# Memory attention in two rounds by token half, with the output projection in three passes, the first among the steps of the second round

## The chip, the cores and the metric

The kernel runs on one core of a Trainium2 chip. The metric is the device time of one launch in microseconds (us); a smaller one is better. A profiled execution gives, besides its own time, every instruction of the engines: PE (TensorE), DVE (VectorE), ACT (ScalarE), POOL (GpSimd), and SP, which issues the DMA transfers.

## The reference

One inference step of a hybrid decoder layer on 1024 prompt tokens and 8 x 4 = 32 sample tokens, 1056 columns in all, with D = 1024. The change concerns the middle of it:

```python
# prompt: mem_k, mem_v of 256 memory tokens computed by memory_kv; sample: cache_mem_k, cache_mem_v
h = rmsnorm(x, norm_mem)
qm = (h @ w_mq).reshape(bsz, seqlen, MEM_HEADS, MEM_HEAD_DIM)          # 4 heads of 256
s = jnp.einsum('blhd,bmhd->bhlm', qm, mem_k).astype(f32) * (MEM_HEAD_DIM ** -0.5)
pr = jax.nn.softmax(s, axis=-1).astype(x.dtype)
o = jnp.einsum('bhlm,bmhd->blhd', pr, mem_v).reshape(bsz, seqlen, D_MODEL)
x = x + o @ w_mo
h = rmsnorm(x, norm_ffn)
u = h @ w_up                                                           # start of the FFN
```

The 1024 prompt tokens share one memory of 256 tokens; each of the 8 sample sequences (4 tokens each) has a cached memory of its own, 2 MB of keys and 2 MB of values in two tiles of 512 KB each.

## The kernel before, in words

Activations lie transposed: channels on the 128 partitions, in eight tiles, tokens along the columns. Each product is made of three matmuls of rounded parts, high x high, high x low, low x high. The high part is written by ACT (`wh`, `s`), the low part by DVE (`wl`, `s`). Weights come in units of 128 x 512 (256 KB): one DMA into a raw tile (`wr`, three buffers), one ACT copy and one DVE subtraction (`wsplit`, L202). A list made ahead (`plains`, L213) fixes their order, and `next_unit` (L274) prepares one unit ahead of the one handed out. `tick` (L292) is called between matmuls and advances generators of side work (`background`), one step in so many ticks. All of it stands in program order on each engine, so that an instruction waits for those ahead of it on its engine. Every operation is issued by one helper, so all rows show line 84 (87 in the changed kernel).

PSUM has eight banks of 512 columns. `psum_mode` (L114) divides them anew for each part of the kernel: `mm` tiles of several banks for wide products, `hm` tiles of two banks with two small tiles `ms` in the attention and the output projection, eight `mb` tiles of one bank in the FFN.

**q.** Eight products (`mm_full`, L325) make q from `w_mq`, the last from 783 us on. Each is scaled by the norm into a tile `t` and split into two tiles (high, low) of 1056 columns. In the last two, K and V of head 0 are loaded and split (`load_kv`, L1065). `mask_q` spreads the sample tokens' q for the eight sequences.

**Attention.** A unit is one head and one half of 512 prompt tokens: scores s (`attn_scores`, L1180: 24 matmuls of 256 columns, then softmax along the memory, with the maximum and the scaling on DVE, the exponential on ACT), transposition t (`attn_tr`, L1198: 8 transposes, then the split), output o (`attn_out`, L1211: 12 matmuls of 512 columns, then the split into `oh`, `ol`). The sample tokens' attention is a generator of 20 steps x (`sample_attn`, L1111), of which 8 have 16 matmuls for scores against the cached keys and 8 have 16 for the outputs with the cached values; its tiles are loaded two steps ahead. The string `ATTN` sets the order of s, t, o, x; units go head by head, both halves of a head in a row, and K/V of the next head are loaded after the first half's scores.

**Output projection.** Two passes over 528 columns each, right half (`rh`, with the sample tokens), then left half (`lh`). Each takes all 16 units of `w_mo`, eight output tiles m of 48 matmuls with 264 columns (2 x 264 share a weight). Then x1 is added on DVE, the sum is stored (`scr_acc`) and squared on ACT, and the squares are added up on POOL. While the second pass runs, the right half's norm and the eight input parts of the FFN are made in the background (`inputs_rh`, L1285).

**FFN start.** `psum_mode(1, 0)`, then the products `up_rh(j)` of right-half inputs with one weight unit each, for the j of `EARLY`, 14 of them, while `inputs_lh` (L1329) makes the left half's inputs and the sums and differences that the later products need.

## Time and profile before

| | us |
|---|---|
| median of 3 runs | 1710.28 (1708.33 to 1710.48) |
| profiled execution | 1703.74 |
| its span | 1701.8 |
| PE busy | 1669.1 (98% of the span) |
| DVE, ACT, POOL busy | 1096.0, 808.1, 213.3 |

The span runs from the first to the last instruction that the profile shows. "Busy" for PE runs to the modelled end of pipelined matmuls. A timeline row's start is measured; the time from the start of one block to that of the next is what a block takes. The stages that the change touches are the end of the q products (to 795 us), the attention (795 to 876), the output projection (876 to 973.5) and the start of the FFN.

### The profile page before, as it was taken

What the parts mean: (1) busy time and instruction counts of PE and PEld (TensorE: products, weight loads), DVE (VectorE), ACT (ScalarE), POOL (GpSimd) and SP (SyncE); (2) the same over time, 40 slices, a digit from 0 to 9 for tenths busy, and PEclk for the clock granted to TensorE, in tenths of its full rate; (3) what the DMA queues carried; (4) which work ended last, traced back from release to release, by engine and by line L of the source; (5) the groups of instructions that cost most, each with busy time, mean ns of one, the idle gap of its engine ahead of it and who ended that gap; (6) DMA issues with size and microseconds to landing.
All of it is one profiled execution on the core that took longest, in us unless ns stands there. A gap on an engine that the chain in (4) does not pass through costs nothing.

```text
span 1701.8 us, 30903 instructions
## 1 busy us (share of the span) xinstructions
PE 1669.1 (98%) x12250; PEld 1600.4 (94%) x12250; DVE 1096.0 (64%) x1728; ACT 808.1 (47%) x1494; POOL 213.3 (13%) x376
## 2 busy tenths in 40 slices
PE   9999999999999999999999999999999999999997
PEld 8899989899889899998789999999999999999997
DVE  7766867787778654434644697847484746466576
ACT  7565533434523443223543465656465555555553
POOL 0110000001002000011001200232223221322210
PEclk9999999999999999999999999999999999999999
DMA  6243355444785654313655542483748373654732
GB/s 216 88 164 85 58 141 111 97 105 105 247 288 192 225 165 135 107 44 106 229 187 177 176 158 82 103 139 93 134 91 141 74 124 73 114 99 89 130 122 103
DMA packets 152162, 226.13 MB, mean 133 GB/s; under 512 B 39873, under 2 KB 77249, under 8 KB 152017
## 3 DMA queue, kind: packets, MB, share of 16 engines
q1 hardware_dynamic: 138192, 198.20, 38.8%
q0 software_dynamic: 13824, 25.96, 11.3%
q8 instruction: 96, 1.57, 0.4%
q14 instruction: 50, 0.40, 0.1%
HBM read 156.22 MB, written 67.89 MB: 132 GB/s over the span
## 4 chain that ended last, share of the span: by engine, by line
PE 84%; DMA 7%; DVE 6%; ACT 2%; issue 1%; SPq 0%; DVEq 0%; ACTq 0%
PE mb L84 40%; PE mm L84 30%; PE hm L84 7%; PE ms L84 6%; DVE s L84 3%; DMA s<-scr_acs 3%; ACT s L84 1%; DVE wl L84 1%; DMA wr<-w_mk 1%; DMA s<-xT 0%; ACT wh L84 0%; DMA ld<-kc 0%; SPq L84 0%; DMA ld<-o_v 0%; DMA wr<-w_mv 0%
## 5 line engine op out<-in xcount | busy, mean ns | idle before, releaser
L84 PE MATMUL mb<-s,wh 128*128 128x264 f32 x3616 | 662.6, 285 | 1.1 <-DVE s L84 0.9
L84 PEld LDWEIGHTS mb<-s,wh 128*128 128x128 f32 x3616 | 560.8, 188 | 1.9 <-ACT wh L84 1.4
L84 PE MATMUL mb<-s,wl 128*128 128x264 f32 x1808 | 511.7, 284 | 0.7 <-DVE wl L84 0.7
L84 PE MATMUL mm<-s,wh 128*128 128x352 f32 (+1 forms) x2624 | 509.1, 326 | 1.1 <-DVE s L84 0.9
L84 PEld LDWEIGHTS mm<-s,wh 128*128 128x128 f32 x2624 | 431.9, 188 | 7.6 <-DVE s L84 2.1
L84 PEld LDWEIGHTS mb<-s,wl 128*128 128x128 f32 x1808 | 340.4, 188 | 1.1 <-DVE wl L84 1.1
L84 ACT ACTIVATE wh<-wr 128x512 fp32r<-128x512 f32 (+1 forms) x252 | 153.3, 608 | 352.0 <-PE mm L84 213.4
L84 PE MATMUL mm<-s,wl 128*128 128x352 f32 (+1 forms) x1312 | 289.2, 322 | 0.6 <-DVE wl L84 0.6
L84 DVE TENSOR_TENSOR wl<-wr,wh 128x512 fp32r<-128x512 f32 (+1 forms) x252 | 167.8, 668 | 125.9 <-ACT wh L84 122.5
L84 PEld LDWEIGHTS mm<-s,wl 128*128 128x128 f32 x1312 | 224.8, 189 | 3.0 <-DVE wl L84 1.2
L84 DVE SCALAR_TENSOR_TENSOR t<-t,par 128x1104 f32<-128x1104 f32 (+4 forms) x132 | 169.6, 1297 | 34.7 <-ACT t L84 33.3
L84 ACT ACTIVATE s<-s 128x512 f32<-128x512 f32 (+8 forms) x138 | 94.1, 690 | 128.4 <-DVE s L84 64.1
L84 DVE TENSOR_TENSOR wl<-ws,wh 128x512 fp32r<-128x512 f32 x118 | 81.0, 689 | 103.9 <-ACT wh L84 103.7
L84 ACT ACTIVATE q<-mb 128x264 f32<-128x264 f32 x264 | 99.7, 384 | 92.5 <-PE mb L84 69.6
L84 POOL DMA_DIRECT2D scr_acc<-q x96 | 83.0, 864 | 198.0 <-ACT q L84 181.5
L84 DVE TENSOR_TENSOR s<-s 128x512 f32<-128x512 f32 (+9 forms) x102 | 82.0, 824 | 32.5 <-ACT s L84 31.1
L84 ACT ACTIVATE wh<-ws 128x512 fp32r<-128x512 f32 x118 | 73.9, 628 | 55.3 <-PE mb L84 49.1
L84 ACT ACTIVATE t<-mb 128x264 f32<-128x264 f32 x132 | 51.2, 389 | 73.6 <-PE mb L84 72.1
L84 PE MATMUL hm<-s,wh 128*128 128x264 f32 x512 | 84.0, 285 | 0.3 <-ACT s L84 0.3
L84 DVE TENSOR_TENSOR t<-mm,rbc 128x1056 f32<-128x1056 f32 (+4 forms) x51 | 45.6, 908 | 52.8 <-PE mm L84 52.2
L84 ACT ACTIVATE t<-t,par 128x1104 f32<-128x1104 f32 (+4 forms) x60 | 74.6, 1247 | 4.7 <-DVE t L84 1.7
L84 PEld LDWEIGHTS hm<-s,wh 128*128 128x128 f32 x512 | 71.1, 188 | 0.7 <-ACT s L84 0.5
(189 smaller groups left out, 1742.0 us busy)
## 6 DMA issues: line engine op xcount, KB each, us to landing
scr_acc<-q POOLq DMA_DIRECT2D x96, 264.0 KB, 4.3
ws<-w_up SPq DMA_DIRECT2D x66, 256.0 KB, 3.1
wr<-w_in SPq DMA_DIRECT2D x56, 256.0 KB, 2.9
wr<-w_up SPq DMA_DIRECT2D x36, 256.0 KB, 2.8
wr<-w_dn SPq DMA_DIRECT2D x48, 192.0 KB, 2.4
s<-scr_acs SPq DMA_DIRECT2D x33, 256.0 KB, 5.2
wr<-w_mo SPq DMA_DIRECT2D x32, 256.0 KB, 2.8
scr_pool<-t SPq DMA_DIRECT2D x8, 528.0 KB, 5.9
```

Source lines behind the costliest of these rows:

```text
L84: i = fn(*args, **kwargs)
```

## The change

**Order of the attention.** Units are ordered by token half: all four heads for prompt tokens 512 to 1023 (`lb` 1) first, then all four for tokens 0 to 511. The string has a fourth letter, m, a step of half an output tile of the projection's first pass. In the first round s and x fill between t and o, in the second m.

**Three passes.** The first pass (`mo_first`) takes the 512 prompt tokens whose outputs the first round has made: 8 tiles of 24 matmuls with 512 columns, as 16 steps m. The output tiles `oh`, `ol` hold these tokens in columns 0 to 511, then the 32 sample tokens, then tokens 0 to 511. The second pass takes columns 512 to 783, the third 784 to 1055, 24 matmuls of 272 columns per tile; the last tile's two units are kept from the second to the third, so that 46 units are loaded instead of 32. x1 comes in one transfer per tile, in the first pass.

**PSUM and buffers.** Eight one-bank `mb` tiles from the attention on, no second change before the FFN; scores, transposes and outputs are evicted bank by bank. High and low part of q lie in one tile per half. K and V of heads 0 to 2 are loaded and split within the last q products, head 3 after the third score unit. The cache tiles come from a table of pools (`CACHE_IN`), three steps ahead instead of two.

**Side work.** The squares are added on DVE instead of POOL. In the third pass only the tiles 4 to 7 of the FFN's right-half inputs are made, 0 to 3 behind it in `inputs_lh`. `EARLY` has one more product.

PE at the opening of the attention, from the last matmuls of the q products (`mm`) on. Sample steps are the groups of 32x256, a transposition 128x128 x8, an output unit 128x512 x12; of a row of sample steps only the beginning is shown. Before:

```order
L84 MATMUL mm<-s,wl 128x352 x3
L84 MATMUL hm<-kv,s 128x256 x24
L84 MATMUL ms<-ld,sq 32x256 x2
L84 MATMUL ms<-ld,s 32x256 x2
...
L84 MATMUL hm<-kv,s 128x256 x24
L84 MATMUL ms<-t,sq 32x256 x2
L84 MATMUL ms<-t,s 32x256 x2
...
L84 MATMUL hm<-cst,p 128x128 x8
L84 MATMUL hm<-s 128x256 x24
```

In the changed kernel:

```order
L87 MATMUL mm<-s,wl 128x352 x3
L87 MATMUL mb<-kv,s 128x256 x24
L87 MATMUL mb<-s 128x256 x24
L87 MATMUL mb<-ld,qm 32x256 x10
L87 MATMUL mb<-s,qm 32x256 x2
...
L87 MATMUL mb<-cst,p 128x128 x8
L87 MATMUL mb<-s 128x256 x24
L87 MATMUL mb<-s,kv 128x512 x12
```

The second score unit has moved ahead of the first sample step, two sample steps stand ahead of the first transposition instead of three, and from there a score unit stands between a transposition and its output unit.

PE at the end of the attention. Before, the last transposition, sample steps, the last output unit, the sample outputs' transposes (`os_`), and the projection's first matmuls (weights `wh`, `wl`):

```order
L84 MATMUL hm<-cst,p 128x128 x8
L84 MATMUL ms<-ld,s 32x256 x8
L84 MATMUL ms<-t,s 32x256 x8
L84 MATMUL hm<-s 128x512 x12
L84 MATMUL ms<-cst,os__8472 128x128 x2
L84 MATMUL hm<-s,wh 128x264 x7
L84 MATMUL hm<-s,wl 128x264 x2
```

In the changed kernel, the beginning of the second round (the fifth unit's output is the row with `kv`, `pm` are the sample tokens' probabilities):

```order
L87 MATMUL mb<-s,wh 128x512 x2
L87 MATMUL mb<-s,wl 128x512
L87 MATMUL mb<-s,kv 128x512 x12
L87 MATMUL mb<-s 128x256 x24
L87 MATMUL mb<-t,pm 32x256 x8
L87 MATMUL mb<-ld,pm 32x256 x8
L87 MATMUL mb<-cst,p 128x128 x8
```

Matmuls of the projection now stand, like sample steps before, between a transposition and the next output unit, and the second round's units and steps stand between matmuls of the projection.

DVE in the projection: the lower parts of the weight units (`wl`) and the adds of x1 (`s<-hm,t`, `s<-mb,s`). Before, at its beginning (128x32 are the sample outputs' low parts):

```order
L84 TENSOR_TENSOR wl<-wr,wh 128x512
L84 TENSOR_TENSOR s<-ms,s 128x32 x2
L84 TENSOR_TENSOR s<-hm,t 128x528
L84 TENSOR_TENSOR wl<-wr,wh 128x512 x2
L84 TENSOR_TENSOR s<-hm,t 128x528
```

In the second pass of the changed kernel:

```order
L87 TENSOR_TENSOR wl<-wr,wh 128x512
L87 TENSOR_TENSOR s<-mb,s 128x32
L87 TENSOR_TENSOR s<-mb,s 128x240
L87 TENSOR_TENSOR wl<-wr,wh 128x512
L87 TENSOR_TENSOR s<-s,t 128x528
L87 TENSOR_TENSOR s<-s,t 128x240
```

The square sums (`s<-s,t`) have come to DVE between the splits, and the add comes in two pieces.

The diff, cut to its core:

```diff
-EARLY = (*range(13), 21)
+EARLY = (*range(14), 21)
-ATTN = "sxsxxt" + "sxoxt" * 3 + "sxotsxotsxot" + "xxoxxtxxxo"
+ATTN = "ssxxtsotxxsotxxsotxxsoxt" + "mxmosxxtmmmosxxtmmmoxxtmmmoxxmxmmxmm"
+CACHE_IN = ("ll", "lS", "SS", "SS", "ll", "lT", "Tl", "ll", "TT", "ll", "lT", "Tl", "ll", "TT", "ll", "lT")
+IN_EVERY = 3
+RH_LAG = 4
-    for nm in ("w_out_y", "w_mq", "w_mo", "w_mo"):
-        plains(A[nm][m, h] for m in range(8) for h in range(2))
+    for nm, n in (("w_out_y", 8), ("w_mq", 8), ("w_mo", 8), ("w_mo", 8), ("w_mo", 7)):
+        plains(A[nm][m, h] for m in range(n) for h in range(2))
...
     for m in range(8):
         if m == 6:
-            load_kv(0)
+            kvr[0] = kv_raw(0)
         ps = mm_full(KT, hh, hl)
+        if m == 6:
+            split_kv(0, kvr[0])
+            kvr[1] = kv_raw(1)
+        if m == 7:
+            split_kv(1, kvr[1])
+            nxt.append(cache(0, 0))
+            kvr[2] = kv_raw(2)
+            split_kv(2, kvr[2])
+            kvr[3] = kv_raw(3)
         t = ttile()
         V.tensor_tensor(v3(t), ps[:, :, :BW], v3(rbs[0]), op=ALU.mult)
...
-        hi, lo = split(t[:, :T])
+        for lb in (1, 0):
+            src = t[:, lb * 512:(lb + 1) * 512]
+            qt[m][lb] = q = stile(F32R)
+            S.activation(q[:, :512], src, AF.Copy)
+            V.tensor_tensor(q[:, 512:1024], src, q[:, :512].bitcast(F32), op=ALU.subtract)
...
-            nxt.append(cache(b >= 6, (b + 2) % 8))
+            nxt.append(cache(b >= 5, (b + 3) % 8))
...
+    def mo_first():
+        for m in range(8):
+            ps = mbtile()
+            mo(ps, 0, slice(0, 512))
+            yield
+            t = stile()
+            dma(t[:, :T], scr["x1"][m])
+            xs.append(t)
+            mo(ps, 4, slice(0, 512))
+            mo_add(m, ps, 0, 512, 512)
+            yield
-    psum_mode(2)
-    aun = [(h, 1 - i) for h in range(4) for i in range(2)]
+    psum_mode(1, 0)
+    aun = [(h, 1 - i) for i in range(2) for h in range(4)]
...
-            u = sq if m == 0 else ttile()
-            S.activation(u[:, o], xs[m][:, c], AF.Square)
-            if m:
-                G.tensor_tensor(sq[:, c], sq[:, c], u[:, o], op=ALU.add)
...
+    def add_squares(m, c, first):
+        if first:
+            S.activation(sq[:, c], xs[m][:, c], AF.Square)
+        else:
+            u = ttile()[:, :c.stop - c.start]
+            S.activation(u, xs[m][:, c], AF.Square)
+            V.tensor_tensor(sq[:, c], sq[:, c], u, op=ALU.add)
+    for m in range(8):
+        ps = mbtile()[:, :272]
+        kept = [mo(ps, k0, slice(512, 784), True) for k0 in (0, 4)]
+        mo_add(m, ps, 0, TP, TS)
+        mo_add(m, ps, TS, 0, 240)
+        dma(scr["acc"][m, 1], xs[m][:, rh])
+        add_squares(m, rh, m == 0)
+        add_squares(m, slice(0, 240), m == 0)
+    background(inputs, IN_EVERY)
+    for m in (7, 0, 1, 2, 3, 4, 5, 6):
+        ps = mbtile()[:, :272]
+        for k0 in (0, 4):
+            mo(ps, k0, slice(784, T), True, kept.pop(0) if kept else None)
+        mo_add(m, ps, 0, 240, 272)
+        dma(scr["acc"][m, 0], xs[m][:, lh])
+        add_squares(m, slice(240, TH), m == 7)
```

## Rows read from the trace of the kernel before

**Rows 1.** Windows by stage of core 0: the attention stage, the two halves of the output projection, the start of the FFN. Columns: from:to and length in us, then for PE, PE's weight load, DVE, ACT and POOL the busy us with the count, then PE's granted clock, the DMA engines' busy share and GB/s.

```profile
794.50:876.00 81.50, 74.18 (x615) 55.92 (x614) 49.28 (x82) 40.94 (x103) 3.04 (x2) 0.98 0.61 211
876.00:924.70 48.70, 48.39 (x395) 47.98 (x394) 18.82 (x35) 16.98 (x33) 7.97 (x6) 1.00 0.54 170
924.70:972.50 47.80, 47.76 (x388) 47.06 (x386) 30.45 (x49) 20.80 (x34) 10.77 (x9) 1.00 0.54 176
972.50:1024.00 51.50, 49.75 (x400) 48.83 (x400) 42.63 (x74) 32.24 (x71) 1.50 (x3) 1.00 0.48 161
```

**Rows 2.** Timeline of PE from the end of the last q product (mm) through the opening of the attention. Columns: start us, us from the first matmul's start to the last one's end, engine, line, operation, out<-in, weights (rows*columns), moving tile, count, and in brackets the idle time before it and what ended it. `hm<-kv,s` and `hm<-s` of 128x256 are score units, `ms<-ld,sq` and `ms<-t,sq` the matmuls of sample steps (the shown row opens each step), `hm<-cst,p` of 128x128 a transposition, `hm<-s,kv` of 128x512 an output unit.

```profile
794.37 0.65 PE L84 MATMUL mm<-s,wl 128*128 128x352 f32 x3
796.43 3.13 PE L84 MATMUL hm<-kv,s 128*128 128x256 f32 x24 [1.42 <-DVE t L84]
...
803.67 0.63 PE L84 MATMUL ms<-t,sq 128*32 128x256 f32 x4
...
807.65 1.03 PE L84 MATMUL ms<-ld,sq 128*32 128x256 f32 x4 [2.61 <-DMA ld<-kc]
...
811.11 1.09 PE L84 MATMUL hm<-cst,p 128*128 128x128 f32 x8
811.96 3.07 PE L84 MATMUL hm<-s 128*128 128x256 f32 x24
814.95 0.41 PE L84 MATMUL ms<-t,sq 128*32 128x256 f32 x2
...
815.95 3.05 PE L84 MATMUL hm<-s,kv 128*128 128x512 f32 x12
```

**Rows 3.** Windows, the stretch behind PE's longest stop in the attention; columns as in rows 1.

```profile
807.65:811.10 3.45, 2.88 (x16) 0.72 (x16) 1.06 (x4) 1.02 (x6) 0.00 (x0) 0.51 0.93 355
```

**Rows 4.** PE's waits in the attention stage, 794 to 876 us. Columns: what PE was to work on, what it waited for, us in total, times, longest us.

```profile
PE ms L84 <- DMA ld<-kc: 3.2, 2, 2.6
PE hm L84 <- DVE t L84: 1.4, 1, 1.4
...
PE ms L84 <- DMA ld<-vc: 0.7, 1, 0.7
```

**Rows 5.** Timeline of PE around the place where the fourth unit's output follows its transposition (836.46, x8); columns as in rows 2. `ms<-cst,p` are the two small transposes of the sample tokens' probabilities, `hm<-s` of 128x512 the output unit, which is interrupted.

```profile
837.25 3.08 PE L84 MATMUL hm<-s 128*128 128x256 f32 x24
840.55 0.44 PE L84 MATMUL ms<-cst,p 128*128 128x128 f32 x2 [0.23 <-ACT p L84]
841.46 0.50 PE L84 MATMUL hm<-s 128*128 128x512 f32 x1 [0.47 <-ACT s L84]
843.14 2.82 PE L84 MATMUL hm<-s 128*128 128x512 f32 x11 [1.18 <-DVE s L84]
845.80 1.04 PE L84 MATMUL hm<-cst,p 128*128 128x128 f32 x8
```

**Rows 6.** Timeline of PE at the first matmul of the output projection, at its end, and at the first matmul of the FFN (`mb`); columns as in rows 2.

```profile
876.04 0.49 PE L84 MATMUL hm<-s,wh 128*128 128x264 f32 x2
...
970.96 0.66 PE L84 MATMUL hm<-s,wh 128*128 128x264 f32 x4
...
971.70 0.66 PE L84 MATMUL hm<-s,wh 128*128 128x264 f32 x4
...
973.49 0.36 PE L84 MATMUL mb<-s,wh 128*128 128x264 f32 x1 [0.89 <-DVE s L84]
```

**Rows 7.** Timeline of PE in an earlier stage (w_mv) whose matmuls have 512 columns; columns as in rows 2.

```profile
594.18 0.63 PE L84 MATMUL mm<-wh,s 128*128 128x512 f32 x2
...
594.88 0.63 PE L84 MATMUL mm<-wh,s 128*128 128x512 f32 x2
```

**Rows 8.** DMA issues between 880 and 960 us. Columns: out<-in, queue, operation, count, KB each, median us from issue to landing.

```profile
wr<-w_mo SPq DMA_DIRECT2D x26, 256.0 KB, 2.8
```

**Rows 9.** Windows, the stage of the 16 units of w_mk (K of the memory tokens); columns as in rows 1.

```profile
554.20:579.14 24.94, 24.11 (x193) 23.09 (x193) 14.25 (x24) 10.16 (x16) 2.46 (x1) 1.00 0.73 234
```

**Rows 10.** The transfers of w_mk's units, 256 KB each, in the view of one tile.

```profile
DMA to landing us min/median/max: 2.8/3.5/4.6
```

**Rows 11.** VectorE's groups by form in the output projection, 876 to 972.5 us. Columns: line, engine, operation, out<-in, shapes, count, busy us and mean ns of one, idle before and its releaser. The first is the lower part of a weight unit's split, the second the add of the projection to x1.

```profile
L84 DVE TENSOR_TENSOR wl<-wr,wh 128x512 fp32r<-128x512 f32 x31 | 22.0, 711 | 22.4 <-ACT wh L84 22.4
L84 DVE TENSOR_TENSOR s<-hm,t 128x528 f32<-128x528 f32 x15 | 10.6, 706 | 19.3 <-PE hm L84 19.3
```

**Rows 12.** ScalarE's groups by form in the same stretch; columns as in rows 11. It is the upper part of a weight unit's split.

```profile
L84 ACT ACTIVATE wh<-wr 128x512 fp32r<-128x512 f32 x32 | 20.2, 631 | 44.4 <-PE hm L84 42.1 <-issue 2.2
```

**Rows 13.** Timeline of VectorE at the start of the FFN; columns as in rows 2 (without weights). The third row is the scaling of five inputs by norm and gain, the fourth six operations on 528 columns each.

```profile
977.63 0.69 DVE L84 TENSOR_TENSOR wl<-wr,wh 128x512 fp32r<-128x512 f32 x1 [3.69 <-ACT wh L84]
...
984.03 0.69 DVE L84 TENSOR_TENSOR wl<-wr,wh 128x512 fp32r<-128x512 f32 x1 [2.23 <-ACT wh L84]
...
985.44 3.48 DVE L84 SCALAR_TENSOR_TENSOR s<-s,par 128x528 f32<-128x528 f32 x5
...
1006.86 3.81 DVE L84 TENSOR_TENSOR s<-s 128x528 fp32r<-128x528 f32 x6
```

**Rows 14.** Timeline of PE in the same stretch, the matmuls that came late; columns as in rows 2.

```profile
1010.58 0.51 PE L84 MATMUL mb<-s,wh 128*128 128x264 f32 x2 [0.16 <-ACT wh L84]
1011.32 0.39 PE L84 MATMUL mb<-s,wl 128*128 128x264 f32 x1 [0.23 <-DVE wl L84]
...
1014.99 0.39 PE L84 MATMUL mb<-s,wl 128*128 128x264 f32 x1 [0.47 <-DVE wl L84]
```

More of the change, by code (lines that the diff above doesn't have):

```diff
@@ L1084, in mask_q, with cache @@
                         mask.unsqueeze(1).to_broadcast([P, 4, 8, TS]), op=ALU.mult)
-    qh, ql = [], []
+    def cache(kv, b):
+        ts = []
+        for i in range(2):
+            t = {"l": ldtile, "T": ttile, "S": stile}[CACHE_IN[8 * kv + b][i]]()
+            dma(t[:, :1024], A["vc"][b, i] if kv else A["kc"][b, :, i * 1024:(i + 1) * 1024])
+            ts.append(t)
+        return ts
+    nxt = deque()
+    qt = [[None, None] for _ in range(8)]
+    kvr = {}
     for m in range(8):
         if m == 6:
-            load_kv(0)
+            kvr[0] = kv_raw(0)
         ps = mm_full(KT, hh, hl)
+        if m == 6:
[7 more added lines that the diff above has]
+            kvr[3] = kv_raw(3)
         t = ttile()
@@ L1180, in attn_scores, with attn_tr, attn_out @@
     def attn_scores(h, lb):
+        kvh, kvl = kvs[h]
+        ps = [mbtile() for _ in range(2)]
+        for q in range(2):
+            for i in range(2):
+                lt = slice((2 * q + i) * P, (2 * q + i + 1) * P)
+                lo = slice(512 + lt.start, 512 + lt.stop)
+                n = 0
+                for dt2 in range(2):
+                    kc = slice(dt2 * 256, dt2 * 256 + 256)
+                    x = qt[2 * h + dt2][lb]
+                    for a, b_ in ((lt, kvh), (lt, kvl), (lo, kvh)):
+                        PE.matmul(ps[q][:, i * 256:(i + 1) * 256], lhsT=x[:, a], rhs=b_[:, kc],
+                                  start=(n == 0), stop=(n == 5))
+                        n += 1
+        return softmax_rows([ps[0], None, ps[1], None])
+    def attn_tr(pts):
+        pth, ptl = stile(F32R), stile(F32R)
+        for mt in range(2):
+            ps = mbtile()
+            for i in range(4):
+                PE.transpose(ps[:, i * P:(i + 1) * P], pts[:, i, mt * P:(mt + 1) * P], ident)
+            c = slice(mt * 512, (mt + 1) * 512)
+            S.activation(pth[:, c], ps, AF.Copy)
+            V.tensor_tensor(ptl[:, c], ps, pth[:, c].bitcast(F32), op=ALU.subtract)
+        return pth, ptl
+    def attn_out(h, lb, pth, ptl):
         if lb == 1:
@@ L1250, in body @@
         else:
-            next(sa)
-    for _ in sa:
-        pass
+            next({"x": sa, "m": mf}[c])
+    for g in (sa, mf):
+        for _ in g:
+            pass
     PE.force = False
@@ L1277, in scaled, with rh_part @@
         V.scalar_tensor_tensor(xs[m][:, c], xs[m][:, c], pc("norm_ffn", m), rb[:, c], op0=ALU.mult, op1=ALU.mult)
-    def norm_half(c):
-        r = norm_cols(sq[:, c], TH, D)
-        yield
-        bc_cols(r, TH, rb[:, c])
-        yield
+    xop = {n: [] for n in ("b11", "b21", "b22", "t1", "t2", "t3", "t4")}
+    def rh_part(m):
+        scaled(m, rh)
+        h = sx.tile([P, T], F32R, tag="S", name="s") if m >= 4 else stile(F32R)
+        parts(h[:, rh], h[:, lh], xs[m][:, rh])
+        xop["b21" if m >= 4 else "b11"].append((h[:, rh], h[:, lh]))
@@ L1285, in inputs_rh @@
     def inputs_rh():
         yield
-        yield from norm_half(rh)
-        for m in range(8):
-            scaled(m, rh)
-            hs[m] = sx.tile([P, T], F32R, tag="S", name="s") if m < 4 else stile(F32R)
-            parts(hs[m][:, rh], hs[m][:, lh], xs[m][:, rh])
+        yield
+        r = norm_cols(sq[:, rh], TH, D)
+        for _ in range(RH_LAG):
+            yield
+        bc_cols(r, TH, rb[:, rh])
+        yield
+        for m in range(4, 8):
+            rh_part(m)
             yield
@@ L1331, in inputs_lh @@
         yield
-        g = norm_half(lh)
-        yield next(g)
-        for _ in range(RL_LAG):
+        r = norm_cols(sq[:, lh], TH, D)
+        for m in range(4):
+            rh_part(m)
             yield
-        yield next(g)
+            yield
+        bc_cols(r, TH, rb[:, lh])
+        yield
         for m in (0, 4, 1, 5, 2, 6, 3, 7):
@@ L1379, in inputs_lh, with banks, hb @@
             yield
+    def add_squares(m, c, first):
+        if first:
+            S.activation(sq[:, c], xs[m][:, c], AF.Square)
+        else:
+            u = ttile()[:, :c.stop - c.start]
[9 more added lines that the diff above has]
+        add_squares(m, slice(0, 240), m == 0)
+    inputs = inputs_rh()
+    background(inputs, IN_EVERY)
[6 more added lines that the diff above has]
+        add_squares(m, slice(240, TH), m == 7)
+    drain()
+    act = {}
+    def banks():
+        return [mbtile() for _ in range(2)]
+    def hb(t, b):
+        return t[:, b * HB:(b + 1) * HB]
     inputs = inputs_lh()
@@ L1385, in o8 @@
         return t[:, TP:T].rearrange("p (b t) -> p b t", b=8)
-    def banks():
-        return [mbtile() for _ in range(2)]
-    def hb(t, b):
-        return t[:, b * HB:(b + 1) * HB]
     def product(name, ps=None, out=None, add=None):
```

144 lines of the change are left out of this document (49 added, 95 removed).

## The prediction

> **What bounds the kernel now.** I read the windows by stage first, then TensorE's timeline in the stages that the change touches, then its list of waits, and last the transfers and VectorE. The windows [rows 1] show one engine at its limit: in the two halves of the output projection PE is busy 48.39 of 48.70 us and 47.76 of 47.80 us at a granted clock of 1.00, in the 51.5 us behind them 49.75. Only the attention stage, 81.5 us long, has holes: 74.18 busy. So time can come from two places alone: holes in PE, and columns that PE need not stream. The timeline of the opening [rows 2] gives the blocks' full pace, start to start: a score unit 2.99 us (811.96 to 814.95), a sample step of 16 small matmuls 1.00 (814.95 to 815.95) or 0.95, a transposition 0.85 (811.11 to 811.96), an output unit 3.0. A hole stands at 804.6: the third sample step should have run to 805.6, waited for a cache tile until 807.65, and the stretch from there to 811.10 ran at a granted clock of 0.51, that is at 1.2 GHz [rows 3]. The list of waits [rows 4] names the rest: the cache tiles, the evacuation of the last q product (DVE t), one more cache tile.
>
> **The sum's base.** Everything below is taken from the profiled execution, 1703.74 us (span 1701.8 and 1.94 around it). The median of the runs shown is 1710.28, 6.54 higher; I carry savings in us to the median.
>
> **Attention before its projection steps.** From the end of the last q product (795.02) [rows 2] to the first projection matmul (876.04) [rows 6] are 81.0 us. Full pace is 8 x 2.99 + 8 x 2.98 + 8 x 0.85 + 16 x 0.95 + 0.4 for four small transposes = 70.1. So 10.9 us are holes: 1.4 at the start, 5.5 at the third step (811.11 - 804.62 = 6.49, less its own 0.95), 2.3 around 841 [rows 5] (from 837.25 a score unit, two small transposes and an output unit want 6.2 and the next block begins at 845.80), 0.75 for a cache tile [rows 4], 0.9 in pieces.
>
> The change keeps the first: the one-bank tiles take over the banks of the q product, and its last tile is still read by VectorE: 1.4. The second goes. Two score units now stand ahead of the first step, K and V of heads 0 to 2 are loaded in the last q products, and cache tiles are asked for three steps ahead; with 6 us of score units ahead of the first step, against the 2.61 us that were missing, I find no load that is last. The half clock came right behind that wait, after PE had stood 2.61 us, and goes with it. The third goes if other work stands in the hole, and it does: in the second round every transposition is followed by projection steps of 12 matmuls of 512 columns (2.8 us) before its output unit. What is late next is the chain from transposition by ACT and VectorE to the output unit, in the first round, where a score unit of 3.0 us covers it. I leave every unit 0.35 us, between the 0.23 and 0.47 of the small waits at 840 to 842 [rows 5]: 8 x 0.35 = 2.8, and 0.3 for the first softmax, which has two score units of cover only. Kept 1.4 + 2.8 + 0.3 = 4.5, **saved 6.4**. Bounds: 9.2 if all but the 1.7 goes, 4 if the chain is long (first rival).
>
> The evictions by bank instead of by pair cost ACT and VectorE one more instruction for each 1024 columns, off PE's path and started half a tile earlier: zero. Moving x1's loads into these steps puts 4.3 MB ahead of the projection's weights on SP's queue; SP asks for them as soon as a tile is free, not when PE comes to the step, and a late one holds VectorE's add while PE has other banks: zero. K/V tiles and masked q in other buffers: zero, no engine does more.
>
> **The output projection.** Before: 768 matmuls of 264 columns, 876.04 to 973.49, 97.45 us. Six take 0.74 us (970.96 to 971.70) [rows 6], 0.122 each, 93.5 in all; about 1.1 for the norm's transposes, 0.89 for the change of PSUM tiles at 973.49, the rest in pieces. After: 8 x 24 = 192 matmuls of 512 columns, and 2 x 8 x 24 = 384 of 272. Three of 512 take 0.70 us [rows 7], 0.233 each: 44.7. 272 columns are between: 0.122 + 8/248 x (0.233 - 0.122) = 0.1255, so 48.2. Sum 92.9, with 1.1 for the transposes and 1.2 for block ends 95.2: **2.2 saved**, the 0.89 in it, since there is no second change of PSUM tiles.
>
> Against this stands the load loop. Before, a weight unit of 24 matmuls lasts 2.9 us; in the second and third pass it lasts 12 x 0.1255 = 1.5 us, with three raw buffers. A buffer comes round in landing + split, the split 0.63 on ACT and 0.71 on VectorE [rows 11, 12], so a unit can come every (L + 1.34)/3. In the projection before, L is 2.8 [rows 8]: 1.38, enough. But traffic rises: two 256 KB units and a 264 KB store per 3.0 us are 258 GB/s, where the windows before show 170 to 176. The nearest stage is the one that loads w_mk: 234 GB/s, a unit every 1.56 us (16 in 24.94), L 3.5 [rows 9, 10]. There (3.5 + 1.34)/3 = 1.61 and 16 units lost 24.94 - 24.11 = 0.83 us of PE [rows 9]. By that rate the 30 units of the two passes lose **1.6**, which I take. Bounds: 0 at L = 2.8, 8 at 4.0, 14 at the 4.6 that w_mk's worst transfer took [rows 10]. The Trainium skill, "SBUF — State Buffer", section "The DMA setup-cost knee", fits a transfer as about 2 us plus its bytes at 436 GB/s; that makes 2.6 us for a unit whatever else is under way, a loop below 1.5, no loss, and 1.6 more saved. The trace disagrees: the same 256 KB took 3.5 as a median there [rows 10].
>
> VectorE also gets closer to its limit. Per block of the second pass it has two splits, an add in two pieces and two square sums that POOL did before: 2 x 0.71 + 0.2 + 0.32 + 0.71 + 0.32 = 2.97 of 3.0 us, the parts of 32 and 240 columns estimated from the 528 of [rows 11]; about 2.7 by the 0.63 that six in a row take each [rows 13]. The third pass has smaller pieces but adds four input parts (0.68 + 0.63 each) and comes to about the same. I charge nothing beyond the 1.6, since PE waits for a split only if VectorE falls a whole unit behind; if it does, the second rival's price applies.
>
> **The start of the FFN.** VectorE runs without a gap from 985 to 1024, and two products began late there: 0.16 + 0.23 and 0.47 of idle [rows 14]. By pace it is more: from 1011.32 to 1014.99 24 matmuls took 3.67 us, 0.74 over 24 x 0.122, and the first, with two stops, lost some 0.9; 1.65 together. The change puts one more early product ahead, 2.9 us more of cover, but moves four of the eight right-half inputs here: 4 x (0.68 + 0.63) = 5.2 us of VectorE. It was idle 3.69 + 2.23 us ahead of 985 [rows 13]; that takes them. I take **0.8 saved**, half, between 0 and 1.65.
>
> Sum: 6.4 + 2.2 - 1.6 + 0.8 = **7.8**, so 1710.28 - 7.8 = 1702.5 (1695.9 for an execution like the profiled one).
>
> **Rivals.** First, the chain behind a transposition is long in the first round too. For: around 841 the transposition ended at 837.25 and the output unit ran freely only from 843.14, 5.8 us [rows 5]; the gaps in the first round are one score unit of 3.0 or with two sample steps 4.9. One such of 2.8 and three of 0.9 are 5.5, so 2.7 above my 2.8: 1705.2, up to 1707. Against: at 815.95 the output unit started without a wait 4.0 us behind its transposition, and eviction by bank shortens the chain. Chance 0.14.
>
> Second, on the slower side: the load loop sets the pace of passes two and three. For: three buffers, 46 units in place of 32, the w_mk stage [rows 9, 10]. Against: the transfers that share the queue there are no larger than 264 KB. At L = 4.0 it costs 30 x (1.78 - 1.505) = 8.2 us, 6.6 more than I took: 1709.1, no gain. From L = 4.1 it is slower than before, and at 4.6 it costs 14: 1715. Chance 0.20, of it 0.02 still faster, 0.08 the same, 0.10 slower.
>
> Third, the clock. PE's clock fell to 1.2 GHz after one stop of 2.61 us, and 3.45 us were then run at half speed, 1.7 lost [rows 3]. More, shorter groups on eight small tiles mean more stops; two falls would be 3.4: 1705.9. The Trainium skill, "TensorE: Matmul & The Clock Gate", section "A second HAM failure mode: psum-queue depth-cycling", tells of a kernel that cycles through PSUM banks and idles between groups often enough for the clock to go up and down. By that rule the change would be hurt; the traces bear it little, for the FFN on one-bank tiles behind 973.49 shows 1.00 [rows 1]. Chance 0.06.
>
> **How the numbers follow.** The forecast, 1702.5, has 0.60; its own range is 1697 (attention saves 9.2, no loss in the loop, 1.65 at the FFN, 13 in all) to 1706. To hold the time 8 times in 10 the range reaches over the first and third rival and the middle of the second: 1697 to 1709. A measurement of this kernel can tell 0.2%, 3.4 us, from no change: faster is below 1706.9, slower above 1713.7. Faster: 0.60 + 0.11 + 0.02 + 0.05 = 0.78; same: 0.03 + 0.08 + 0.01 = 0.12; slower 0.10.
>
> **What would show it.** Right: the attention stage with its 16 sample steps, eight units and 192 projection matmuls in some 74.6 + 44.7 = 119 us between the last q product and the first matmul of 272 columns; no wait for a cache tile; no window there below a clock of 0.95; passes two and three in 49 to 52 us with w_mo landing below 3.5. Wrong: units of passes two and three 1.6 us apart or more with ACT waiting for wr (second rival), PE waiting on DVE s in the first round (first), a clock near 0.5 in several windows (third), or late products again at the head of the FFN.

## The result, and the profile after

| us | before | changed |
|---|---|---|
| median of 5 runs | 1710.28 (1705.02 to 1710.64) | 1697.74 (1694.95 to 1701.03) |
| profiled execution, its span | 1703.74, 1701.8 | 1699.94, 1698.2 |

The ratio is 0.9937 with a 95% interval of 0.9917 to 0.9957, that is 7 to 14 us less. The change makes the kernel faster; the 7.8 us forecast lie within the interval, near its lower end. The spans of the two profiled executions lie only 3.6 us apart, since they also differ in stages that the change doesn't touch: the last q product ended at 795.01 before and at 798.38 after. So the stages are compared by their lengths, from the timelines: from the end of the last q product to the first projection matmul and to the first FFN matmul (before) or to the first matmul of 272 columns and the first FFN matmul (after), and to the end of the span.

| us | before | changed |
|---|---|---|
| attention (changed: with the first pass, 44.7 at pace) | 81.0 | 119.1 |
| projection (changed: second and third pass) | 97.4 | 24.6 + 27.2 |
| FFN to the end | 728.3 | 728.9 |
| sum from the last q product | 906.8 | 899.8 |

That is 7.0 us less in this pair: 6.7 in the attention without the first pass (119.1 - 44.7 = 74.4), 0.9 in the projection with it (44.7 + 51.8 = 96.5), 0.6 lost in the FFN. The first pass stands among the steps of the attention and can't be timed by itself, so its 44.7 is the length of its 192 matmuls at pace, not a measurement.

The windows of the changed kernel, columns as in [rows 1]:

```profile
798.00:809.50 11.50, 8.14 (x83) 6.72 (x81) 8.86 (x14) 5.84 (x16) 3.50 (x2) 1.00 0.82 305
809.50:815.00 5.50, 5.45 (x33) 5.45 (x34) 3.21 (x9) 3.69 (x10) 0.00 (x0) 0.69 0.89 358
815.00:845.00 30.00, 29.71 (x249) 23.63 (x248) 17.82 (x40) 15.28 (x49) 0.00 (x0) 1.00 0.45 147
845.00:917.45 72.45, 72.45 (x447) 57.42 (x446) 36.57 (x70) 26.17 (x63) 0.00 (x0) 1.00 0.59 200
917.45:942.05 24.60, 24.60 (x194) 24.22 (x192) 18.80 (x41) 15.39 (x29) 0.00 (x0) 1.00 0.70 217
942.05:969.26 27.21, 26.35 (x204) 25.30 (x203) 24.08 (x53) 16.32 (x30) 0.79 (x4) 1.00 0.71 220
```

The second round, 845.00 to 917.45, has no hole at all: PE is busy in all of its 72.45 us. All but 0.3 us of what is left of the attention's holes lies in the first 17 us, and there the clock fell once more, to a mean of 0.69 over 5.5 us. PE's waits, as in [rows 4]:

```profile
PE mb L87 <- ACT p L87: 2.0, 1, 2.0
PE mb L87 <- DVE t L87: 1.4, 1, 1.4
PE mb L87 <- DMA ld<-kc: 0.3, 1, 0.3
```

The start's 1.4 us has stayed, 3.2 us for kc have become 0.3, the wait for vc and the stops around the fourth output unit [rows 5] are gone. New are 2.0 us for ACT. The timeline of the opening, as in [rows 2]:

```profile
799.80 3.10 PE L87 MATMUL mb<-kv,s 128*128 128x256 f32 x24 [1.42 <-DVE t L87]
802.73 2.96 PE L87 MATMUL mb<-s 128*128 128x256 f32 x24
805.63 1.27 PE L87 MATMUL mb<-ld,qm 128*32 128x256 f32 x18
...
809.55 1.10 PE L87 MATMUL mb<-cst,p 128*128 128x128 f32 x8 [1.99 <-ACT p L87]
810.40 4.60 PE L87 MATMUL mb<-s 128*128 128x256 f32 x24
814.84 2.95 PE L87 MATMUL mb<-s,kv 128*128 128x512 f32 x12
817.63 1.03 PE L87 MATMUL mb<-cst,p 128*128 128x128 f32 x8
```

The first transposition waits 1.99 us for its probabilities, and the score unit behind it takes 4.44 us, to 814.84, where the first two take 2.9: 1.5 more, the half clock. The stop comes at the end of a chain that is to be read on VectorE, POOL and ACT:

```profile
800.44 3.49 DVE L87 TENSOR_TENSOR s<-t,s 128x512 fp32r<-128x512 f32 x2
803.86 1.28 DVE L87 TENSOR_REDUCE mx<-mb 128x2 f32<-128x512 f32 x2
```

```profile
800.50 2.89 POOL L87 TENSOR_TENSOR qm<-qs,maskt 128x1024 f32<-128x1024 f32 x1
```

```profile
805.42 1.28 ACT L87 ACT_TABLE_LOAD   x1 [4.48 <-DVE mx L87]
```

Two subtractions of 512 columns take 3.49 us on VectorE, where 1.3 would be usual, while POOL spreads the sample tokens' q: the first has its 0.69, the second takes 2.88 beside POOL's 2.89. The maxima wait behind them on VectorE, the load of ACT's table for the exponential behind the maxima, the exponentials behind that.

### The profile page after: what moved, and what is told of

Read it like the earlier page. It is cut to its first block, busy times and chain, and to the rows that moved or that the text cites. A ratio compares the mean times of both kernels' runs of the same rounds, so it can differ in the third digit from the quotient of the medians.

```text
span 1698.2 us, 30613 instructions
## 1 busy us (share of the span) xinstructions
PE 1665.7 (98%) x12058; PEld 1591.3 (94%) x12058; DVE 1114.4 (66%) x1802; ACT 816.7 (48%) x1534; POOL 203.1 (12%) x362
## 4 chain that ended last, share of the span: by engine, by line
PE 84%; DMA 6%; DVE 6%; ACT 2%; issue 1%; SPq 0%; DVEq 0%; POOL 0%; ACTq 0%
PE mb L87 48%; PE mm L87 31%; PE ms L87 6%; DVE s L87 3%; DMA s<-scr_acs 2%; DVE wl L87 1%; DVE t L87 1%; DMA wr<-w_mv 1%; ACT s L87 1%; ACT wh L87 1%; DMA s<-xT 0%; DMA ld<-kc 0%; SPq L87 0%; DMA ld<-h0T 0%; DMA ld<-scr_pool 0%
## 5 line engine op out<-in xcount | busy, mean ns | idle before, releaser
L87 PE MATMUL mb<-s,wh 128*128 128x264 f32 (+2 forms) x4000 | 750.9, 288 | 0.3 <-ACT wh L87 0.3
L87 PEld LDWEIGHTS mb<-s,wh 128*128 128x128 f32 x4000 | 624.8, 188 | 6.3 <-ACT wh L87 0.7
L87 PE MATMUL mb<-s,wl 128*128 128x264 f32 (+2 forms) x2000 | 574.6, 288 | 1.9 <-DVE wl L87 1.8
L87 PEld LDWEIGHTS mb<-s,wl 128*128 128x128 f32 x2000 | 376.0, 188 | 6.5 <-DVE wl L87 3.5
L87 ACT ACTIVATE wh<-wr 128x512 fp32r<-128x512 f32 (+1 forms) x267 | 162.7, 609 | 348.5 <-PE mm L87 190.2
L87 DVE TENSOR_TENSOR wl<-wr,wh 128x512 fp32r<-128x512 f32 (+1 forms) x267 | 177.1, 665 | 116.4 <-ACT wh L87 114.7
L87 ACT ACTIVATE s<-s 128x512 f32<-128x512 f32 (+9 forms) x141 | 96.2, 691 | 131.0 <-DMA s<-scr_acs 64.4
L87 PE MATMUL mb<-s 128*128 128x256 f32 (+2 forms) x504 | 85.4, 327 | 0.0
L87 PEld LDWEIGHTS mb<-s 128*128 128x128 f32 x504 | 78.9, 193 | 3.9 <-ACT s L87 0.4
```

What stands on the lines that cost most here:

```text
L87: i = fn(*args, **kwargs)
```

## The experiments

Runs with rounds have a ratio to the kernel before; of the others the stages of one profile are read. Lengths are from the end of the last q product to the first matmul of 272 columns ("attention"), 119.1 in the changed kernel, unless another stretch is named.

**Is the kernel before steady?** Two more profiles of it (no edit).

> The kernel before, unchanged, profiled once more. The two profiles at hand differ by 7.0 us from the end of the last q product on, and the medians by 12.5. Theory A (the medians' rest is spread between executions, in stages that both kernels share): from the last q product to the end it takes 905 to 908 us again, as the first profile's 906.8, and the time ahead of it differs by some us. Rival B (the attention before is itself unsteady, and the first profile caught a good execution): the stop for the third cache tile is longer than 2.6 us or there are more of them, and the stretch from the last q product to the first projection matmul is 84 us or more instead of 81.0.

> The kernel before, a third profile. From the last q product to the first projection matmul the first took 81.0 us and the second 85.9. Theory B (the attention before is unsteady, its cache waits and the clock behind them differ between executions): a third length between 81 and 88 us, the difference from 81.0 made of waits for kc and vc and of stretches at a clock near 0.5. Rival (one of the two was an accident): 81.0 or 85.9 within 0.3 us and the same waits.

The attention, here to the first projection matmul, took 85.9 and 82.3 us after 81.0 in the first profile; from the last q product to the end it was 912.3 and 907.8, against 906.8. The waits in the second profile, then in the third:

```profile
PE ms L84 <- DMA ld<-kc: 4.5, 2, 2.5
PE ms L84 <- DMA ld<-vc: 1.6, 1, 1.6
```

```profile
PE ms L84 <- DMA ld<-kc: 3.0, 2, 2.1
PE ms L84 <- DMA ld<-vc: 1.7, 1, 1.7
```

In the second profile the clock fell behind the waits for kc, for longer than in [rows 3], and once more at the fourth output unit, where it stops as in [rows 5]:

```profile
812.90:819.00 6.10, 6.02 (x32) 4.74 (x33) 1.11 (x1) 1.42 (x2) 0.00 (x0) 0.51 0.81 299
847.00:853.00 6.00, 4.83 (x15) 3.56 (x15) 4.73 (x9) 2.77 (x10) 0.00 (x0) 0.72 0.01 4
```

Rival B holds: the attention before is unsteady, by its cache waits (3.9, 6.1 and 4.7 us in sum) and by whether half clock follows a stop, and the profile that I predicted from was the best of three. (Theory A held in part too: the time ahead of the attention differed by 2 to 3 us.)

**The steps of the first pass moved behind the attention.**

```diff
-ATTN = "ssxxtsotxxsotxxsotxxsoxt" + "mxmosxxtmmmosxxtmmmoxxtmmmoxxmxmmxmm"
+ATTN = "ssxxtsotxxsotxxsotxxsoxt" + "xosxxtosxxtoxxtoxxxx" + "m" * 16
```

> The changed kernel with all 16 half steps of the projection's first pass behind the attention instead of between its second round's steps; the same work. Theory (what the steps bring is cover: they stand between a transposition and its output unit, and between the sample steps and their loads): four output units of the second round stand bare behind their transpositions, 2 to 2.8 us each, and the value tiles are asked for at twice the rate, so 8 to 14 us more than the changed kernel, falls of the clock among it. Rival (the gain is the 512 columns of the first pass, 24 matmuls per tile instead of 2 x 24): the time is the changed kernel's within 1.5 us.

Attention 127.7 us, 8.6 more, and the second and third pass 52.6, 0.8 more; ratio 1.0003 (0.9990 to 1.0016). With the cover goes as much time as the whole change had gained. The first of PE's stops in its second round:

```profile
846.23 0.44 PE L87 MATMUL mb<-cst,p 128*128 128x128 f32 x2 [1.73 <-ACT p L87]
848.58 4.12 PE L87 MATMUL mb<-s,kv 128*128 128x512 f32 x11 [1.37 <-DVE s L87]
859.01 0.50 PE L87 MATMUL mb<-s 128*128 128x512 f32 x1 [0.61 <-ACT s L87]
860.24 5.71 PE L87 MATMUL mb<-s 128*128 128x512 f32 x35 [0.74 <-DVE s L87]
869.45 0.50 PE L87 MATMUL mb<-s 128*128 128x512 f32 x1 [0.62 <-ACT s L87]
870.69 2.82 PE L87 MATMUL mb<-s 128*128 128x512 f32 x11 [0.74 <-DVE s L87]
```

The fifth unit's transposition waits for ACT, and every output unit of the round waits for the split behind its transposition, by VectorE or by ACT and then VectorE; the one with kv runs 4.12 us, with half clock in it. No cache tile was waited for: the loads, which I had among the causes, were not one. This kernel is not the kernel before again, though it takes the same time. It has no waits for the cache, but less cover in the second round: three of its four output units follow their transposition at once, where before a score unit or sample steps stood between. So the run shows what the projection's steps are worth as cover in this order, and not that the whole gain is cover.

**What took the cache wait away: the order or the earlier request?** Two steps ahead instead of three:

```diff
-    nxt.extend(cache(0, b) for b in (1, 2))
+    nxt.extend(cache(0, b) for b in (1,))
...
-            nxt.append(cache(b >= 5, (b + 3) % 8))
+            nxt.append(cache(b >= 6, (b + 2) % 8))
...
-            if b < 5:
-                nxt.append(cache(1, b + 3))
+            if b < 6:
+                nxt.append(cache(1, b + 2))
```

> The changed kernel with cache tiles asked for two steps ahead, as before, instead of three. Theory (the two score units ahead of the first sample step removed the wait, the third step ahead is not needed): waits for kc and vc below 0.6 us in sum, the attention as long as with three, 119 us within 0.7. Rival (asking three ahead removed it): a wait of 1.5 us or more for a cache tile in the first round, half clock behind it, 122 us or more.

And the first two steps as before, one behind each of the first two score units:

```diff
-ATTN = "ssxxtsotxxsotxxsotxxsoxt" + "mxmosxxtmmmosxxtmmmoxxtmmmoxxmxmmxmm"
+ATTN = "sxsxtsotxxsotxxsotxxsoxt" + "mxmosxxtmmmosxxtmmmoxxtmmmoxxmxmmxmm"
```

> The changed kernel with the first two sample steps standing as before, one behind each of the first two score units, instead of both behind the second; the third step stays where the change put it. Theory G (the order took the cache wait away: before, three steps stood within 8 us of the start): no wait for kc, the same stop of about 2 us ahead of the first transposition, 117 to 119 us to the first matmul of 272 columns. Rival H (the first tile set comes only just in time for the changed order): a wait for kc of 0.5 us or more at the first step, and above 119 us.

Neither has a wait for a cache tile in the attention. It took 117.0 and 116.6 us, less than 119.1 mainly because no half clock followed the first transposition's stop (1.95 and 0.95 us). So neither the third step ahead nor the place of the first two steps is needed by itself; what both kernels share is that the third step stands behind a transposition, a score unit, an output unit and another transposition, some 10 us later than before, and that K and V are loaded in the q products. Which of these two suffices wasn't tried.

**The stop ahead of the first transposition.** The spreading on POOL in two pieces, three quarters of it meant for the seventh product's end:

```diff
...
-        if m % 4 == 3:
-            mask_q()
+        if m == 3:
+            mask_q(0, 0, 4)
+        elif m == 6:
+            mask_q(1, 0, 3)
+        elif m == 7:
+            mask_q(1, 3, 4)
```

> The changed kernel with the spreading of the sample tokens' q on POOL cut in two: for three of the last four tiles right behind the seventh q product, for the last one behind the eighth, the same elements in all. Theory (PE's stop of 1.99 us ahead of the first transposition comes from a VectorE subtraction that took 2.88 us beside POOL's 2.89 us operation, where its twin took 0.69, and the half clock behind the stop comes from the stop): the subtraction takes about 0.7 to 1.2 us, the stop shrinks to 0.3 or less, no stretch at a clock near 0.5 follows, and the span from the last q product to the first matmul of 272 columns goes from 119.1 to about 116. Rival (the subtraction waits for something else, or the ACT table load and the exponentials alone hold the softmax): the stop stays above 1.5 us, 119 us.

Attention 116.3 us, the stop 1.26, clock 1.00 behind it; ratio 0.9933 (0.9918 to 0.9947), not to be told from the changed kernel's. The edit did only a part of what it should: POOL's larger piece waited for the last q product all the same, 11.10 us, since its tile takes the buffer of the norm's factors, and the stop stayed above the 0.3 expected.

```profile
800.51 2.16 POOL L87 TENSOR_TENSOR qm<-qs,maskt 128x768 f32<-128x768 f32 x1 [11.10 <-DVE t L87]
```

```profile
801.06 2.77 DVE L87 TENSOR_TENSOR s<-t,s 128x512 fp32r<-128x512 f32 x2
```

With a POOL operation 0.73 us shorter the pair of subtractions is 0.72 shorter, and the stop 0.73. The next kernel takes POOL out altogether, by a VectorE operation behind the first unit's maxima in `softmax_rows`, and the table load out of the chain:

```diff
...
+        if len(qm) == 1:
+            V.force = True
+            mask_q(V)
+            V.force = False
...
+    S.force = True
+    S.activation(dum, maskt[:, :4], AF.Exp)
+    S.force = False
     psum_mode(1, 0)
```

> The changed kernel with two edits at the opening of the attention: the second half of the spreading of the sample tokens' q is done by VectorE behind the first unit's maxima instead of by POOL beside VectorE's subtractions, and an exponential of 4 columns stands on ACT ahead of the first softmax, so that the table is loaded while ACT is idle. Theory (the stop ahead of the first transposition is the sum of a subtraction held up by POOL, about 2.2 us, and the table load, 1.28): both subtractions take 0.7 us, the stop falls from 1.99 to below 0.3, the clock stays at 1.00, and from the last q product to the first matmul of 272 columns there are 115.5 to 116 us instead of 119.1. Rival (the exponentials wait for the maxima of a score unit that is itself late): the stop stays above 1 us.

```profile
799.68 1.29 DVE L87 TENSOR_TENSOR s<-t,s 128x512 fp32r<-128x512 f32 x2
```

```profile
804.90 1.27 PE L87 MATMUL mb<-ld,qm 128*32 128x256 f32 x18
...
806.77 1.09 PE L87 MATMUL mb<-cst,p 128*128 128x128 f32 x8
807.62 3.09 PE L87 MATMUL mb<-s 128*128 128x256 f32 x24
```

The two subtractions take 1.29 us, the stop is gone, and the attention takes 114.9, 4.1 less than in the changed kernel's first profile: the theory holds. (Two edits are in this run at once; POOL's part is shown by the run before, the table load's share isn't measured by itself.) The ratio, 0.9930 (0.9908 to 0.9952), shows nothing of it; this execution's FFN was 2.4 us longer, 1.2 of it behind its last matmul of 264 columns, of which more below, and 1.2 that no run here explains.

**The passes: VectorE or the load loop?** The sums of squares back on POOL:

```diff
-            V.tensor_tensor(sq[:, c], sq[:, c], u, op=ALU.add)
+            G.tensor_tensor(sq[:, c], sq[:, c], u, op=ALU.add)
```

> The changed kernel with the sums of squares of the second and third pass on POOL again, as before; the same sums. Theory D (VectorE's load costs the passes some 1 us and the head of the FFN 1.4): the second and third pass go from 51.8 to about 51.0 us and the first 20 products of the FFN, 58.7 us, get 0.5 to 1 shorter. Rival L (the load loop holds the passes, and the FFN's head waits for its own sums and differences): both unchanged within 0.2 us. Rival P (VectorE is held up when POOL works beside it): the passes get longer, above 52.3.

The passes took 25.4 + 28.0 us, 1.6 more, and the first products of the FFN, to the start of the 20th, 59.9, 1.2 more. The second pass's 0.8 lies within what it varies by over the runs with no edit to it (24.1 to 25.5). The third pass's 0.8 does not (27.0 to 27.3 in the others, but for the 28.2 with the steps behind the attention, where one stop of 1.5 us for ACT stands in it), nor does the FFN's 1.2. VectorE's lower parts in the passes (917 to 970 us), first of the changed kernel, then of this one:

```profile
L87 DVE TENSOR_TENSOR wl<-wr,wh 128x512 fp32r<-128x512 f32 x29 | 20.0, 688 | 6.4 <-ACT wh L87 6.0
```

```profile
L87 DVE TENSOR_TENSOR wl<-wr,wh 128x512 fp32r<-128x512 f32 x28 | 22.3, 798 | 11.7 <-ACT wh L87 11.3
```

Rival P: a subtraction takes 798 ns instead of 688 in the mean while POOL adds beside it. VectorE has less to do and is slower. It reaches PE in two places: VectorE's last operation of the norm, on 5 columns, took 0.76 us beside a POOL sum instead of 0.16, and PE's stop ahead of the norm's transposes is 0.80 us instead of 0.20; at the FFN's start PE stops 0.95 us for a subtraction that took 1.28. That the change takes these sums from POOL is a gain that I had at nothing, as far as one profile shows it.

**More raw buffers for the third pass.** Six of the FFN's pool, asked for five units ahead:

```diff
...
+    plains((A["w_mo"][m, h] for m in range(7) for h in range(2)), 5, stmp)
```

> The changed kernel with the 14 weight units of the third pass loaded into the six raw buffers of the FFN's pool, asked for five units ahead, instead of three buffers two ahead; the same loads. Theory L (the load loop costs the third pass time): the third pass goes from 27.2 us to 26.5 or less and ACT no longer waits for w_mo in it. Rival D (VectorE sets it): unchanged within 0.2 us, with VectorE's lower parts late as before.

ACT's waits in the third pass of the changed kernel include the following row; in this kernel's there is none for w_mo:

```profile
ACT wh L87 <- DMA wr<-w_mo: 3.2, 4, 1.3
```

Yet the third pass took 27.0 us, against 27.2 and 27.1 in two profiles of the changed kernel. The loads were late for ACT, but not for PE; the loop does not set the third pass.

**The head of the FFN.** One early product fewer:

```diff
-EARLY = (*range(14), 21)
+EARLY = (*range(13), 21)
```

> The changed kernel with 13 + 1 early products at the head of the FFN instead of 14 + 1, as before; the product left out there is made with its group later. The FFN, from its first product to the end, took 728.3 us before and 728.9 changed; the changed kernel has a stop of 0.84 us at the 33rd product that the one before lacks, and its head gained nothing. Theory E (the extra early product is what covers the four input parts that moved behind the projection): without it the first 20 products get 1 us or more longer than 58.7. Rival F (VectorE's lag there is the same with or without, since one product's time is one product's splits): the first 20 products stay within 0.3 us, and the stop at the 33rd product goes, so that the FFN is back at 728.3 or less.

To the start of the 20th product (the 58.7 us of the expectations are these 19 products) it took 59.2 us, 0.5 more: between the two. PE's late products, first two of the changed kernel, then this kernel's:

```profile
1013.76 0.39 PE L87 MATMUL mb<-s,wl 128*128 128x264 f32 x1 [0.48 <-DVE wl L87]
...
1067.17 0.39 PE L87 MATMUL mb<-s,wl 128*128 128x264 f32 x1 [0.68 <-DVE wl L87]
```

```profile
1009.99 0.39 PE L87 MATMUL mb<-s,wl 128*128 128x264 f32 x1 [1.69 <-DVE wl L87]
```

The extra product is worth half a us there. The stop at 1067.17, at the 33rd product, is gone, as the rival had it. It stands, 0.68 to 0.81 us long, in eight of the ten profiles of kernels with 14 + 1 early products (not in the changed kernel's second one, nor in the one with the steps as before) and in none of the four with 13 + 1, three of them the kernel before. So what the extra product saves at the head, 0.5 us, is mostly lost again there.

**The best version, and the changed kernel again.** The two edits of the opening together with the third pass's buffers, and the changed kernel once more.

> The changed kernel with the two edits at the opening of the attention (the spreading by VectorE behind the first maxima, the exponential's table ahead) and the third pass's weight units in the FFN's raw buffers, five ahead. By the stages of the runs so far: 115.0 us to the first matmul of 272 columns instead of 119.1 or, where no half clock follows the stop, 117; the second and third pass 51.1 to 51.6 instead of 51.8; so 2.5 to 4.5 us less than the changed kernel in the stages. The median should be 2 to 4 us below that of the changed kernel in the same job, near the noise of single executions, and 12 to 15 below the kernel before.

> The changed kernel, unchanged, on the same chip. From the last q product to the end it took 899.8 us in its first profile, and the kernel before 906.8, 912.3 and 907.8 in three. Theory B (the median's 12.5 us are 7 to 9 us of stages that the change touches, more where the kernel before loses more at its cache waits, and the rest is spread between executions): 898 to 901 us from the last q product on, and a ratio to the kernel before of 0.993 to 0.996.

The changed kernel: 1699.28 us (1697.88 to 1703.28), ratio 0.9933 (0.9916 to 0.9950); from the last q product on 898.1 us, the attention 116.7, the passes 24.7 + 27.1, the FFN 729.5. It had the same stop of 1.96 us, and no half clock behind it:

```profile
809.50:815.00 5.50, 5.32 (x39) 5.06 (x40) 4.33 (x11) 3.81 (x11) 0.00 (x0) 1.00 0.92 358
```

The best version: 1697.31 us (1694.34 to 1698.63), ratio 0.9917 (0.9899 to 0.9934), attention 114.6, passes 24.6 + 27.0. It beats the kernel before by 11 to 17 us; against the changed kernel the medians differ by 2.0, the lower end of what was expected, but the intervals overlap, so that the runs don't settle it, while the stages do for the attention (114.6 and 114.9 against 116.7 and 119.1).

## Why the prediction was right, point by point

**What bounds.** Holes in PE's attention, as put: nearly all of the gain lies there. By PE's waits the largest part is the cache: 3.9, 6.1 and 4.7 us in the three profiles before, 0.3 and nothing in the two of the changed kernel, and the half clock behind these waits with them. The projection's steps are needed as cover in the new order, 8.6 us without them; no run has the one without the other, so that the shares are read from waits and not from an experiment.

**Attention, forecast 6.4.** In the pair of profiles 6.7, over all profiles more: (81.0 + 85.9 + 82.3)/3 = 83.1 before, (74.4 + 72.0)/2 = 73.2 after, 9.9. The mechanism was right, in that the cache wait, the clock behind it, and the hole at the fourth unit went; the size was off on both sides. What was to be removed is larger as a rule than in the one execution that I read. What was to remain was put together wrongly: 8 x 0.35 for the units' chains measured nothing, since all eight output units start without a wait, and 0.3 for the first softmax measured 1.99 and at times 1.5 for the clock. The step that failed is "two score units of cover only": I took the softmax's length, and not what stands ahead of it on VectorE, a subtraction slowed by POOL, nor the table load, which [rows 2] hid behind the cache wait. So the sentence that no window would lie below a clock of 0.95 was wrong for the first profile. That 6.4 came out near the pair's 6.7 is luck: 2.8 too much for the chains stood against some 3.2 too little for the first softmax.

**Projection, forecast 2.2 - 1.6 = 0.6.** 0.9 measured, with the first pass at its pace of 44.7. But the load loop's 1.6 was not there in the third pass (e_ws). The second and third pass took 51.8 us, 1.3 more than the 48.2 of their columns with the 2.3 for transposes and block ends. So a loss of about the size I had taken was there for another reason, and that the sum came out is luck in part. PE's waits in the two passes show VectorE's splits, which I charged nothing beyond the loop:

```profile
PE mb L87 <- DVE wl L87: 0.6, 2, 0.5
PE mb L87 <- DVE nr L87: 0.2, 1, 0.2
```

What made up the rest of the 1.3 isn't shown. The landing was 3.4 us in the median of the second pass's transfers and 3.0 in the third, between the 2.8 and 3.5 that I chose from, at 217 and 220 GB/s instead of the 258 I had reckoned (which, with 1024 bytes to the KB, should have been 264). By pass, then over all 46 transfers:

```profile
wr<-w_mo SPq DMA_DIRECT2D x15, 256.0 KB, 3.4
```

```profile
wr<-w_mo SPq DMA_DIRECT2D x11, 256.0 KB, 3.0
```

```profile
DMA to landing us min/median/max: 2.5/3.0/8.2
```

The 2.6 us that I estimated for such a transfer by the Trainium skill, "SBUF — State Buffer", section "The DMA setup-cost knee", is near the fastest of the 46 and not their median; its result, no loss in the load loop, is what the third pass showed.

**FFN's start, forecast 0.8.** Wrong: to the start of the 20th product it took 58.7 us before and after, and the FFN's whole length was 728.0 to 728.9 against 728.9 and 729.5. The four input parts that moved here ate what the extra product covers (e_early13: 0.5), and the stop at the 33rd product, 0.68 in the first profile, is about the 0.6 lost in the pair.

**Rivals.** The chains in the first round (first rival) cost nothing. The load loop (second) didn't set the pace: not of the third pass (e_ws), and the second ran within 0.5 us of its columns' 24.1. The clock (third) fell, as that rival had it, behind one stop of 2 us, but not from shorter groups: the second round on eight one-bank tiles ran 72.45 us at 1.00. The rule of the Trainium skill, "TensorE: Matmul & The Clock Gate", section "A second HAM failure mode: psum-queue depth-cycling", speaks of idling between the groups; PE had none there, so this trace shows only that the small tiles by themselves brought no fall.

**The sum.** 7.8 forecast, 12.5 by the medians, 10.8 by the ratio (0.63% of 1710.28). Mean lengths from the last q product: (906.8 + 912.3 + 907.8)/3 = 909.0 before, (899.8 + 898.1)/2 = 898.9 after, 10.0 less: 9.9 attention, 0.9 projection, -0.8 FFN. Against the forecast's 6.4, 0.6 and 0.8 that is 3.5 and 0.3 us more and 1.6 less. The attention's 3.5 come from its usual executions: those before took 2.1 us more in the mean than the one that I read, those after 1.2 less than their first profile. With three and two profiles this is an estimate. The profiled executions of before took 1703.74, 1712.19 and 1707.03 us, so that the 6.54 between the first and the median lie between executions, 1 to 5 of them in the attention; ahead of it the three differ by up to 3 us, and no run here tells why.

## What to carry to other kernels

Work that needs nothing from a chain, here matmuls of the next product, is worth most between a transposition and the unit that reads it; the same work moved behind the stage cost 8.6 us here. A hole covers what waits behind it: when it goes, read the next chain with everything that stands ahead on each of its engines, among it a table load and operations that another engine holds up. And a profile is one execution: when a stage has waits on transfers, profile it twice before its holes are priced.

## What was not expected of the hardware

**A stop of about 2 us may be followed by half clock, or not.** The stop of 1.95 to 2.0 us ahead of the first transposition stands in seven profiles (the changed kernel's two, steps behind the attention, two steps ahead, POOL sums, six buffers, 13 products); in two of them, the changed kernel's first and the one with 13 products, the clock fell. Ahead of the last norm's transposes all 14 profiles have the same stop of 1.92 us, and in seven of them half clock follows. Two executions, of the changed kernel and of the one with the opening mended; PE's row, which reads alike in both, and the windows behind it:

```profile
1660.67 0.70 PE L87 MATMUL mb<-cst,nr 128*128 128x128 f32 x4 [1.92 <-DVE nr L87]
```

```profile
1660.70:1665.00 4.30, 4.30 (x24) 4.10 (x25) 1.73 (x4) 0.54 (x1) 0.00 (x0) 1.00 0.00 0
```

```profile
1657.00:1661.50 4.50, 4.50 (x18) 4.30 (x19) 0.67 (x2) 0.00 (x0) 0.00 (x0) 0.63 0.00 0
```

From the FFN's last matmul of 264 columns to the end there are 65.2 to 65.8 us with the fall and 63.7 to 64.2 without. That is some 1.5 us by which executions and the FFN's length differ, and the profiles of all three kernels with a mended opening happened to pay it. At the opening a stop of 1.26 and one of 0.95 us were followed by full clock in the one run each has.

**VectorE beside POOL.** A subtraction of 512 columns takes 0.69 us alone; a pair takes 1.29 alone, 2.77 beside a POOL operation of 2.16 and 3.49 beside one of 2.89. In both pairs it is one subtraction that is held, for 2.15 and 2.88 us, about as long as the POOL operation lasts, while the other has its 0.69.
